# Rotary shuffle by transfers or by VectorE, and five smaller moves around it, in a hybrid decoder layer on one core

## The chip, the core and the metric

The kernel runs on one core of a Trainium2 chip. The core has five engines with instruction streams of their own: TensorE (PE: matrix products; PEld is its weight load), VectorE (DVE), ScalarE (ACT), GpSimd (POOL) and SyncE (SP, which here only issues DMA transfers). Each engine works through its instructions in order; semaphores order the engines among each other. SBUF is the memory of 128 partitions that engines work in, PSUM the small one that TensorE writes to. The metric is the device time of one execution in microseconds; less is better.

## The reference

One inference step of a one-layer decoder, for a prompt of 1024 positions and a sample group of 8 x 4 positions, with d = 1024. In short:

```python
xn = rms_norm(x, g_pre_mix)
h = xn @ w_in          # q_a k_a v_a | q_r k_r v_r | gate_r | gm_a gm_r
o_a = window_attn(rope_partial(q_a), rope_partial(k_a), v_a)      # window 128, sinks
qr, kr = rope_ret(q_r), rope_ret(k_r) * DK_R ** -0.5              # 4 heads, key 128, value 256
o_r, new_s = retention(qr, kr, v_r, s0)                           # chunks of 128, decaying state
y_a = o_a @ w_a_proj
y_r = (silu(gate_r) * head_rms(o_r)) @ w_r_proj
mixed = (sigmoid(gm_a) * y_a + sigmoid(gm_r) * y_r) @ w_o
x = x + rms_norm(mixed, g_post_mix)
f = conv_ffn(rms_norm(x, g_pre_ffn))                              # w_up, causal conv of 3, gelu * b, w_down
x = x + rms_norm(f, g_post_ffn)

def rope_ret(x, pos):
    ...
    x1 = x[..., ::2]
    x2 = x[..., 1::2]
    rot = jnp.stack([-x2, x1], axis=-1).reshape(x.shape)
    return x * cos + rot * sin
```

All is float32. Outputs are the new x of both groups, the last 128 keys and values, the retention states and the last two rows of the convolution's input.

## The kernel before

**Numbers and products.** Activations lie transposed, features on the partitions and the T = 1056 positions (32 of the sample, 1024 of the prompt) along the rows. A float32 product is made of three fast ones: both factors are split into a rounded part and a remainder (`split`, L228 on ScalarE for the rounded part, L223 on VectorE for the rest), and `mm3` (L255 to L257) multiplies high by high, high by low and low by high. The large products use Strassen's scheme in Winograd's form, seven quarter products (A11, A12, A22, S1 to S4) in place of eight; the sums of quarters it needs are made on VectorE. HW = T / 4 = 264 columns is a quarter's width.

**Order.** The program is written in the order of the text, but the framework orders each engine's instructions by a simulated timeline (`schedule_with_timeline_sim=True`) and their dependencies. `pin` keeps an instruction in program order with the other pinned ones; `PIN[0] = True` pins all splits. Transfers are issued by SyncE (`ld`) or GpSimd (`st`). `tpool` holds 16 tiles of (128, T), `wsp` three buffers each for `w_hi` and `w_lo`, `wraw` two raw weights.

**Stages**, with their times in the profiled execution:

- 0 to about 250: input norm, attention, the value projection of the retention.
- about 250 to 300: `attn_proj` (L779 to L787), the output projection of the attention; beside it `x_sums(0)` and `x_sums(1)` (L796) build the operands S2, S3, A22 and S1's of both halves of X for the input projection, and `first_weights` (L834) splits five of the first seven weights between the operand S2 and the operands S3 and A22 of half 1; these last are pinned. Then the pool `p2` is closed and `rs` opened in its place.
- `stream` (L901): a generator for the seven products of 16 pairs of column blocks of w_in, each for two halves of the positions. `adv(n)` takes n products of it; other stages call `adv` to mix their work with it. A22's product is made one half late. Each finished half (`pair`, a tile of (128, T): the two blocks beside each other) is handed to a `post`, which runs at `flush` after the S2 product of the next half.
- 300 to about 420, the sample stage: 18 products ahead, then `sample(h)` (L1024 to L1075) for the four heads, three products after each of its five parts. It reads the rotated q and k back from DRAM (`qk_d`), updates the states of the 8 sequences (`s0`, read by SyncE and written by GpSimd) and ends with two transposes (`turn`, L1012) of the normed result. The `post` of the first four pairs is `post_qk`, the retention's rotation: with q or k as x, `x * rcos + shuffled(x) * rsin`, where the shuffle swaps neighbouring partitions (L864), for two blocks of 128 x 528 a half.
- 420 to about 700, the prompt's retention: 32 blocks (`ahead`, `front`, `middle`, `tail`), four products of the stream in each. q and k of a block are loaded four blocks ahead (`load_qk`), five buffers. `tail` also makes eight quads of sums of w_r (`quad_load`, `quad_sums`), two for each head, at blocks 0, 2 and 3, 5, and writes them to `r_d`.
- 700 to about 803: the products with w_r, in the order PORD = A11, A12, S2, S3, A22, S1, S4. `z_done` (L1270) adds the results up in `Gr`, and `merge` (L1260) multiplies a finished quarter by its gate and adds the attention's part (L1267, L1268): GpSimd for row blocks 0 to 3, VectorE for 4 to 7. `merged_to_X` splits `Gr` back into X for half 0 after A22 and for half 1 at the end. In between the eight row blocks of w_o are loaded and split (`weights`, L246 and L223), blocks 2 to 6 into tiles of `tpool`, block 7 into `wsp`.
- 803 to about 918: the output projection w_o with its norms, nine row tiles; row tile 0 takes the blocks of w_o in the order LATE.
- 918 to the end: the FFN, pairs of w_up, convolution, gate, sums of w_down (`down_sums`) and products with w_down.

`NSPL` counts the split weights of a stream: each seventh goes to a tile of its own (`w7x`), the others alternate between the rings `hi` and `lo`.

The seam of the input projection in the text (L819 to L856), as far as the change touches it:

```python
    def x_sums(j):
        ...
        for p, src in ((S2, t2), (S3, t3), (A22, t)):
            if j and p == S3:
                first_weights()
                PIN[0] = True
            ex1[p, j] = [TT("ex", (P, 4, HW), F32R) for _ in range(2)]
            split(*ex1[p, j], src)
        PIN[0] = False
```

## Time and profile before

| what | us |
|---|---|
| median of 3 runs (1672.16 to 1676.08) | 1675.57 |
| the profiled execution | 1673.6 |
| its span, first to last instruction of the program | 1671.8 |

The profile is one execution. A group of instructions is given as line, engine, operation, tile written and tiles read, shape and count, then busy time, mean of one in ns, and the idle time of the engine before them with what ended it. A wait is given as who waited for whom, with the sum, the number and the longest. Idle time of an engine that does not set the pace costs nothing, and one that waits for several things is put down to the last.

### The profile page before, as it was taken

The page shows a single profiled execution, that of the slowest core. Times are in us where ns is not written, and L with a number is a line of the kernel's source. Part 1 is how long each engine was busy: PE and PEld are TensorE (multiplying, and loading weights), DVE is VectorE, ACT ScalarE, POOL GpSimd, SP SyncE. Part 2 cuts the span into 40 slices and gives each one's busy share as a digit, 9 for nine tenths or more (in the row PEclk, how much of TensorE's full clock was granted, in tenths as well). Part 3 has the DMA queues.
Part 4 walks back from the last instruction along what each step waited for, and adds up shares of the span by engine and source line. Part 5 has one row for each costly group of instructions (what it writes and reads, how often), then busy time and mean ns, then how long its engine had stood idle before and what let it go on. Part 6 is the DMA issues. An engine that isn't in the chain of part 4 may idle for free.

```text
span 1671.8 us, 32491 instructions
## 1 busy us (share of the span) xinstructions
PE 1629.8 (97%) x12551; PEld 1587.6 (95%) x12551; DVE 1229.3 (74%) x2035; ACT 860.4 (51%) x1882; POOL 474.1 (28%) x686
## 2 busy tenths in 40 slices
PE   8999999898999999999999999999999999999997
PEld 7999989888999999999688999999999999999997
DVE  7887738799556566478847988888898988455476
ACT  6565634355655655554333655555555556443343
POOL 4242430456343433250412122212322223111111
PEclk9999999999999999999999999999999999999999
DMA  7312232445676775597523144545444548866664
GB/s 199 67 46 72 70 78 99 151 137 170 211 243 217 239 236 178 186 296 213 186 89 103 51 142 159 172 147 172 159 160 160 173 158 257 243 192 195 195 187 144
DMA packets 273291, 273.88 MB, mean 164 GB/s; under 512 B 23040, under 2 KB 234272, under 8 KB 273121
## 3 DMA queue, kind: packets, MB, share of 16 engines
q1 hardware_dynamic: 239377, 155.25, 32.0%
q0 software_dynamic: 33760, 116.57, 20.1%
q8 instruction: 98, 1.61, 0.4%
q14 instruction: 56, 0.46, 0.1%
HBM read 184.24 MB, written 87.49 MB: 163 GB/s over the span
## 4 chain that ended last, share of the span: by engine, by line
PE 68%; DVE 3%; DMA 2%; issue 1%; ACT 1%; SPq 0%; POOL 0%; DVEq 0%; ACTq 0%; POOLq 0%
PE ps_m L257 9%; PE ps_m L256 9%; PE ps_m L255 9%; PE ps_t L256 8%; PE ps_t L255 8%; PE ps_t L257 8%; PE ps_q L255 4%; PE ps_q L257 4%; PE ps_q L256 4%; DVE xl L223 1%; DMA zt<-in_w_r_proj 1%; PE ps_b L1155 1%; PE ps_a L1159 1%; PE ps_b L1157 1%; PE ps_t L461 0%
## 5 line engine op out<-in xcount | busy, mean ns | idle before, releaser
L255 PE MATMUL ps_q<-xh,w 128*128 128x264 f32 x512 | 152.4, 298 | 5.4 <-DVE pair L949 3.0
L223 DVE SCALAR_TENSOR_TENSOR w_lo<-w_raw,w_hi 128x1024 fp32r<-128x1024 f32 x83 | 106.7, 1290 | 65.5 <-ACT w_hi L228 59.9
L255 PE MATMUL ps_t<-xh,w_hi 128*128 128x264 f32 (+2 forms) x524 | 149.0, 284 | 0.0
L256 PE MATMUL ps_t<-xl,w_hi 128*128 128x264 f32 (+2 forms) x524 | 148.9, 284 | 0.0
L257 PE MATMUL ps_t<-xh,w_lo 128*128 128x264 f32 (+2 forms) x524 | 148.2, 283 | 0.0
L257 PE MATMUL ps_m<-xh,w_lo 128*128 128x264 f32 x512 | 145.7, 285 | 0.5 <-DVE w_lo L223 0.5
L255 PE MATMUL ps_m<-xh,w_hi 128*128 128x264 f32 x512 | 146.0, 285 | 0.0
L256 PE MATMUL ps_q<-xl,w 128*128 128x264 f32 x512 | 145.9, 285 | 0.0
L256 PE MATMUL ps_m<-xl,w_hi 128*128 128x264 f32 x512 | 145.5, 284 | 0.0
L257 PE MATMUL ps_q<-xh,w 128*128 128x264 f32 x512 | 145.4, 284 | 0.0
L223 DVE SCALAR_TENSOR_TENSOR w<-w_raw,w 128x512 fp32r<-128x512 f32 x152 | 113.3, 751 | 36.9 <-ACT w L331 35.4
L1500 DVE SCALAR_TENSOR_TENSOR c_out<-u_ext,fconst,c_out 128x1024 f32<-128x1024 f32 x96 | 122.3, 1281 | 2.0 <-ACT c_out L1496 0.5
L228 ACT CAST w_hi<-w_raw 128x1024 fp32r<-128x1024 f32 x62 | 65.2, 1052 | 104.5 <-PE ps_t L256 75.0
L331 ACT CAST w<-w_raw 128x512 fp32r<-128x512 f32 x152 | 93.9, 622 | 37.9 <-DVE w_raw L223 22.9
L255 PEld LDWEIGHTS ps_q<-xh,w 128*128 128x128 f32 x512 | 96.6, 189 | 7.5 <-DVE pair L949 4.4
L257 PEld LDWEIGHTS ps_t<-xh,w_lo 128*128 128x128 f32 x524 | 98.8, 189 | 0.0
L255 PEld LDWEIGHTS ps_t<-xh,w_hi 128*128 128x128 f32 x524 | 98.7, 188 | 0.0
L256 PEld LDWEIGHTS ps_t<-xl,w_hi 128*128 128x128 f32 x524 | 98.7, 188 | 0.0
L257 PEld LDWEIGHTS ps_m<-xh,w_lo 128*128 128x128 f32 x512 | 96.4, 188 | 0.8 <-DVE w_lo L223 0.7
L256 PEld LDWEIGHTS ps_q<-xl,w 128*128 128x128 f32 x512 | 96.6, 189 | 0.5
L256 PEld LDWEIGHTS ps_m<-xl,w_hi 128*128 128x128 f32 x512 | 96.3, 188 | 0.0
L255 PEld LDWEIGHTS ps_m<-xh,w_hi 128*128 128x128 f32 x512 | 96.3, 188 | 0.0
(447 smaller groups left out, 6045.7 us busy)
## 6 DMA issues: line engine op xcount, KB each, us to landing
w_raw<-in_w_up SPq DMA_DIRECT2D x48, 512.0 KB, 4.1
w_raw<-in_w_in SPq DMA_DIRECT2D x42, 512.0 KB, 4.6
w_raw<-s_d SPq DMA_DIRECT2D x60, 256.0 KB, 4.0
t_d<-t POOLq DMA_DIRECT2D x24, 528.0 KB, 3.9
t<-t_d POOLq DMA_DIRECT2D x24, 528.0 KB, 5.1
t<-in_w_down SPq DMA_DIRECT2D x48, 256.0 KB, 4.4
s_d<-t POOLq DMA_DIRECT2D x24, 512.0 KB, 3.5
w_raw<-in_w_down SPq DMA_DIRECT2D x36, 256.0 KB, 5.7
```

The costliest lines, as they stand in the source:

```text
L223: pinned(V.scalar_tensor_tensor(out=out, in0=in0, scalar=1.0, in1=in1, op0=mult, op1=op))
L228: pinned(S.copy(out=hi, in_=src))
L255: TE.matmul(ps, wh, xh, start=start, stop=False, **kw)
L256: TE.matmul(ps, wh, xl, start=False, stop=False, **kw)
L257: TE.matmul(ps, wl, xh, start=False, stop=stop, **kw)
L331: S.copy(out=t[:, 0:4], in_=src)
L1155: TE.matmul(po, sT, vt, start=True, stop=tt == 0)
L1157: TE.matmul(po, q, state["s"], start=False, stop=True)
L1159: TE.matmul(pk, kt, vt, start=True, stop=True)
L1500: V.scalar_tensor_tensor(out=c[:, NS:], in0=u[:, g, NU + t:NU + t + SEQ], scalar=sc[t], in1=c[:, NS:], op0=mult, op1=add)
```

## The change

1. **Rotation.** In `post_qk` the two shuffles of VectorE become four transfers of SyncE inside SBUF, each of 64 of the 128 partitions (even to odd, odd to even), and the two elementwise instructions for each block that GpSimd did are done by VectorE.
2. **Start of the stream.** `first_weights` goes. `x_sums(1)` ends before the operands S3 and A22; four products of the stream are issued first, then these two operands (pinned), and then the pool is closed. In the first pair the weights of S3 and A22 are asked for after the products of S4 and S3. The ring of split weights is shifted by two (`NSPL` 2, and back to 0 for the FFN).
3. **Sums of w_r.** Four of the eight quads, those of column blocks 0 and 1, are made after `x_sums(1)` in two tiles of `p2`; `tail` makes one quad for each head.
4. **Sample stage.** 14 products ahead (with the four above, 18). The last copy of `sample`, with its two transposes, is issued after the next three products, the last one after two.
5. **Retention.** q and k are loaded three blocks ahead.
6. **Seam to w_o.** `merge` runs on VectorE for half 1 and on GpSimd for half 0. w_o's block 6 is split into `wsp` after the last w_r weights, ahead of block 7. Row tile 0 takes the blocks in plain order.
7. **FFN.** Four of the sums of w_down use the tile `t0` in place of `t2`.

```diff
-    NSPL = [0]
+    NSPL = [2]
...
         for p, src in ((S2, t2), (S3, t3), (A22, t)):
             if j and p == S3:
-                first_weights()
-                PIN[0] = True
-            ex1[p, j] = [TT("ex", (P, 4, HW), F32R) for _ in range(2)]
-            split(*ex1[p, j], src)
-        PIN[0] = False
+                return t3, t
+            operand(p, j, src)
+
+    def operand(p, j, src):
+
+        ex1[p, j] = [TT("ex", (P, 4, HW), F32R) for _ in range(2)]
+        split(*ex1[p, j], src)
...
     x_sums(0)
-    x_sums(1)
-
-    ph_stack.close()
-    rp = pool("rs", 1, stack=ph_stack)
+    late = x_sums(1)
+    for n in range(4):
+        t = quarters(p2.tile([P, T], F32, name="quad", bufs=2))
+        quad_load(w_r, n // 2, 0, n % 2, t)
+        quad_sums(r_d, n // 2, 0, n % 2, t)
...
             for i in range(2):
-                V.stream_shuffle(sh[i], both(o)[:, i], R_SHUF)
+                x = both(o)[:, i]
+                for b in range(2):
+                    ld.dma_start(out=sh[i][b::2], in_=x[1 - b::2])
             for i in range(2):
                 x = both(o)[:, i]
-                ew(G, x, x, c, mult)
+                ew(V, x, x, c, mult)
                 ew(V, sh[i], sh[i], d, mult)
-                ew(G, x, x, sh[i], add)
+                ew(V, x, x, sh[i], add)
...
-        ws = begun.pop()
-        ops = dict(begun)
-        ops[S3] = next(ws)
+        ws = in_split(ORDER[0])
+        next(ws)
+        next(ws)
+        ops = {p: next(ws) for p in EARLY[:5]}
...
-                        if j == 0:
+                        if j == 0 and i:
                             ops[A22] = next(ws)
...
+                    if p == S4 and S3 not in ops:
+                        ops[S3] = next(ws)
+                    if p == S3 and A22 not in ops:
+                        ops[A22] = next(ws)
+                        ws = coming
+                        next(ws)
...
+    adv(4)
+    PIN[0] = True
+    for p, t in zip((S3, A22), late):
+        operand(p, 1, t)
+    PIN[0] = False
+    ph_stack.close()
+    rp = pool("rs", 1, stack=ph_stack)
...
-        S.copy(out=z8[:, h], in_=turn(pt, finish(os8, NS, 1, h, 1)))
+        o = finish(os8, NS, 1, h, 1)
+        turns.append(lambda: S.copy(out=z8[:, h], in_=turn(pt, o)))
 
+    turns = []
     for n in range(2):
         load_s0(n)
-    adv(18)
+    adv(14)
     for h in range(4):
         for _ in sample(h):
             adv(3)
+            while turns:
+                turns.pop()()
+    adv(2)
+    turns.pop()()
...
-        if tt in (0, 3):
+        if tt == 0:
             quads[h] = quarters(ST("zt", (P, T), bufs=3))
-            quad_load(w_r, h, 0, tt // 3, quads[h])
-        if tt in (2, 5):
-            quad_sums(r_d, h, 0, tt // 3, quads.pop(h))
+            quad_load(w_r, 2 + h // 2, 0, h % 2, quads[h])
+        if tt == 2:
+            quad_sums(r_d, 2 + h // 2, 0, h % 2, quads.pop(h))
...
-        load_qk(g + 4)
+        load_qk(g + 3)
...
-        eng = G if m < 4 else V
+        eng = V if half else G
...
+    def out_weights(m):
+
+        wo.append(weights(1, D, [(lambda r: r[:, 0], w_o[m * P:(m + 1) * P, :])],
+                          [wop, wop, tpool, tpool, tpool, tpool, None, None][m]))
...
+            if pi == 6 and c == 0:
+                out_weights(6)
...
-        for m in {0: (0,), 1: (1,), 2: (2,), 3: (3, 4), 4: (5,), 5: (6,), 6: (7,)}.get(pi, ()):
-            wo.append(weights(1, D, [(lambda r: r[:, 0], w_o[m * P:(m + 1) * P, :])],
-                              [wop, wop, tpool, tpool, tpool, tpool, tpool, None][m]))
+        for m in {0: (0,), 1: (1,), 2: (2,), 3: (3, 4), 4: (5,), 6: (7,)}.get(pi, ()):
+            out_weights(m)
...
-    LATE = (0, 1, 2, 3, 4, 7, 5, 6)
+    LATE = range(KD)
...
+    NSPL[0] = 0
     prepare(2)
...
-            down_sums(20 + (i - 5) // 4, tr.tile([P, 4, HW], F32, name="t2"))
+            down_sums(20 + (i - 5) // 4, tr.tile([P, 4, HW], F32, name="t0"))
```

More of the change, by code (lines that the diff above doesn't have):

```diff
@@ L793, in trunk @@
     COLS += [(c, c + P) for b in (GR0, GA0, GM0) for c in range(b, b + D, 2 * P)]
-    begun = []
     def x_sums(j):
@@ L832, in in_split @@
         yield w_split(a22, V)
-    def first_weights():
-        ws = in_split(ORDER[0])
-        next(ws)
-        next(ws)
-        begun.extend((p, next(ws)) for p in EARLY[:5])
-        begun.append(ws)
     for mm in range(4):
@@ L1217, in ahead @@
             state["dm"] = mask(g // NB)
-        load_qk(g + 4)
+        load_qk(g + 3)
         load_v(g + 3)
         return front(g, state["dm"])
-    for g in range(4):
+    for g in range(3):
         load_qk(g)
@@ L1225, in trunk @@
         load_v(g)
+    adv(0)
     coming, behind = ahead(0), None
@@ L1239, in trunk @@
     tail(*behind)
-    adv(len(ORDER) * 14 - 8 - 78 - 4 * NBLK - 1)
+    adv(len(ORDER) * 14 - 8 - 80 - 4 * NBLK - 1)
     for n in range(4):
```

## The prediction

> **What bounds the kernel now.** I read the page first, then the stages (busy time of each engine in stretches of the span), then in the stages with an idle TensorE the waits, the groups of instructions and the timeline.
>
> ```profile
> span 1671.8 us, 32491 instructions
> PE 1629.8 (97%) x12551; PEld 1587.6 (95%) x12551; DVE 1229.3 (74%) x2035; ACT 860.4 (51%) x1882; POOL 474.1 (28%) x686
> ```
>
> TensorE is busy for 97%, and the change adds and removes no matmul. So it can win only idle TensorE time, 42 us in all, and only where it lies in stages that the change touches. The stages (stretch, length, busy us and count of PE, PEld, DVE, ACT, POOL, then clock and DMA):
>
> ```profile
> 250.00:300.00 50.00, 48.40 (x314) 48.18 (x314) 36.97 (x37) 22.61 (x41) 4.87 (x9) 1.00 0.24 91
> 300.00:420.00 120.00, 107.04 (x835) 101.86 (x836) 109.78 (x164) 58.98 (x159) 66.99 (x55) 1.00 0.50 157
> 420.00:700.00 280.00, 279.12 (x2161) 273.47 (x2160) 163.99 (x348) 161.54 (x392) 96.90 (x161) 1.00 0.68 213
> ...
> 800.00:820.00 20.00, 16.01 (x62) 12.43 (x61) 18.24 (x27) 8.13 (x20) 11.31 (x9) 0.91 0.71 213
> ...
> 920.00:1660.00 740.00, 740.00 (x6109) 739.61 (x6107) 575.79 (x907) 383.46 (x711) 156.99 (x262) 1.00 0.55 172
> ```
>
> Two places matter. The sample stage, 300 to 420, leaves TensorE idle for 120 - 107.0 = 13.0 us while VectorE is busy for 109.8 of 120: VectorE sets the pace. The seam between the w_r products and the w_o products, 800 to 820, leaves 4.0 us. The FFN (920 to 1660) has nothing to win and 164 us of slack on VectorE. TensorE's waits in the sample stage, then those around the seam (who waited for whom: us, times, longest):
>
> ```profile
> PE ps_b L1062 <- DVE s0s L223: 4.2, 7, 0.8
> PE ps_q L255 <- DVE pair L949: 3.0, 2, 1.8
> PE ps_q L255 <- ACT pair L926: 2.3, 1, 2.3
> PE ps_q L255 <- DVE pair L951: 2.1, 3, 0.9
> PE ps_b L1012 <- ACT o L1006: 1.3, 1, 1.3
> PE ps_a L1041 <- ACT r L1034: 1.0, 1, 1.0
> ```
>
> ```profile
> PE ps_m L256 <- DVE w_loT L223: 3.9, 1, 3.9
> ...
> PE ps_m L257 <- DVE w_lo L223: 0.5, 1, 0.5
> ```
>
> 9.3 of the first 13.9 us are waits for VectorE.
>
> **Term 1, the rotation (sample stage).** `post_qk` runs eight times (four heads, two halves), all of them in this stage. VectorE's groups here, and POOL's (count, then busy us, mean ns, idle before):
>
> ```profile
> L223 DVE SCALAR_TENSOR_TENSOR w<-w_raw,w 128x512 fp32r<-128x512 f32 x17 | 21.2, 1263 | 0.8 <-ACT w L331 0.8
> L223 DVE SCALAR_TENSOR_TENSOR sh<-sh,rsin 128x528 f32<-128x528 f32 x16 | 18.7, 1167 | 0.1
> L864 DVE STREAM_SHUFFLE sh<-pair 128x528 f32<-128x528 f32 x16 | 12.1, 758 | 0.0
> L223 DVE SCALAR_TENSOR_TENSOR s0s<-s,s0s 128x512 fp32r<-128x512 f32 x13 | 10.9, 841 | 0.0
> ...
> L223 DVE SCALAR_TENSOR_TENSOR w<-s,w 128x512 fp32r<-128x512 f32 x9 | 7.3, 812 | 1.2 <-ACT w L331 1.1
> ...
> L223 DVE SCALAR_TENSOR_TENSOR s<-w_raw 128x512 f32<-128x512 f32 x5 | 3.4, 689 | 3.8 <-DMA w_raw<-in_w_in 3.8
> ```
>
> ```profile
> L225 POOL TENSOR_TENSOR pair<-pair,sh 128x528 f32<-128x528 f32 x16 | 25.5, 1596 | 12.4 <-DVE sh L223 12.2
> L225 POOL TENSOR_TENSOR pair<-pair,rcos 128x528 f32<-128x528 f32 x16 | 25.1, 1567 | 28.1 <-DVE sh L864 20.3 <-DMA rcos<-in_rcos 7.8
> ```
>
> The same two shapes in the middle of the FFN, 1000 to 1300:
>
> ```profile
> L223 DVE SCALAR_TENSOR_TENSOR w<-w_raw,w 128x512 fp32r<-128x512 f32 x59 | 40.5, 686 | 7.9 <-ACT w L331 7.9
> ...
> L223 DVE SCALAR_TENSOR_TENSOR t<-c_out,t 128x528 f32<-128x528 f32 x16 | 11.2, 700 | 0.0
> ```
>
> One VectorE instruction that takes 700 ns there takes 1167 ns here. The timeline shows why; VectorE, then POOL:
>
> ```profile
> 321.78 0.70 DVE L223 SCALAR_TENSOR_TENSOR sh<-sh,rsin 128x528 f32<-128x528 f32 x1
> ...
> 324.73 1.82 DVE L223 SCALAR_TENSOR_TENSOR sh<-sh,rsin 128x528 f32<-128x528 f32 x1
> ```
>
> ```profile
> 324.22 1.77 POOL L225 TENSOR_TENSOR pair<-pair,rcos 128x528 f32<-128x528 f32 x1
> ```
>
> The first runs with POOL free; the second starts 0.51 us into a POOL instruction and ends 0.56 us after it. POOL's elementwise work holds up VectorE instructions that read two operands from SBUF. The excess in the quoted groups is 17 x (1263 - 686) = 9.8, 16 x (1167 - 700) = 7.5, 13 x (841 - 686) = 2.0 and 9 x (812 - 686) = 1.1, together 20.4 us, or 0.64 us for each of POOL's 32 instructions.
>
> The change takes POOL's 32 instructions away and does them on VectorE: +32 x 0.700 = +22.4. The 16 shuffles go: -12.1. The excess goes: -20.4. VectorE falls from 109.8 to 99.7 us. Beside its present idle time of 120 - 109.8 = 10.2 us that makes 109.9 us, close to TensorE's own 107.0.
>
> What it adds is a wait. Each post issues four transfers on SyncE (32 in all), SBUF to SBUF, 64 partitions and 132 KB each, and its VectorE instructions, the product with cos included since it overwrites what the transfers read, cannot start before they land. VectorE takes its instructions in order, so what is queued behind, the weight splits (`w_split`) and the evictions at L949 and L951, waits too, and TensorE for those. The trace of before has no such transfer; the nearest ones, and the load that VectorE meets in this stage (KB each, median us to landing):
>
> ```profile
> kS<-kS POOLq DMA_DIRECT2D x8, 96.0 KB, 2.8
> ...
> w_raw<-in_w_in SPq DMA_DIRECT2D x42, 512.0 KB, 4.6
> ```
>
> VectorE's wait is bounded below by nothing (other work stands ahead of it) and above by what it loses to the w_r quads in the next stage, quoted under term 3: 13.5 us in 6 waits, 2.25 each. Nearest is the load of w_raw here, 3.8 us over five first uses, 0.76 each, landing in 4.6 against 2.8; I take 0.5 a post, 4.0 us, and put half of it into idle time that exists already. The stage becomes 109.9 + 2.0 = 111.9: **-8.1 us**. Ends: -13.0 (all idle gone) to +7.9 (2.25 a post, none hidden: 109.9 + 18.0 - 120).
>
> Inside these 13.0 us lie two other parts. The 2.3 us for `ACT pair` fall where ScalarE casts the S3 and A22 operands of half 1 before it evicts; they now come after four products. The 1.3 us for `ACT o` are a sample transpose, now three products later. I count neither again. S3's and A22's own first weights now stand behind S4 and S3 in program order; the attention projection is the cover, and its loss is a rival below.
>
> **Term 2, the seam.** ScalarE at the cast of w_o block 6, and the stage just before:
>
> ```profile
> 806.13 1.05 ACT L246 CAST w_hiT<-w_raw 128x1024 fp32r<-128x1024 f32 x1 [2.77 <-DVE xl L223]
> ```
>
> ```profile
> 780.00:800.00 20.00, 20.00 (x155) 19.39 (x154) 20.00 (x40) 6.01 (x14) 3.57 (x2) 1.00 0.81 238
> ```
>
> Block 6 has tiles of the T pool, so its cast waits for a split of the merged rows, and TensorE 3.9 us for the pair. The change gives it buffers of the ring that the w_r weights use, free before the last products. Block 7 is then late next: it needs the buffer of the next to last w_r weights, but TensorE asks for it only as the last of eight. I take 3.4 of the 4.0 us idle: **-3.4 us**; ends 0 and -4.0. Two of the ring's three buffers stay taken until the last w_o product, so the second w_up weight of the first FFN pair splits late: 1.05 (the cast above) and 1.29 us,
>
> ```profile
> L223 DVE SCALAR_TENSOR_TENSOR w_lo<-w_raw,w_hi 128x1024 fp32r<-128x1024 f32 x83 | 106.7, 1290 | 65.5 <-ACT w_hi L228 59.9
> ```
>
> hidden by the first weight's 96 products at 740 / 6109 = 0.121 us, 11.6 us; without that cover +2.3.
>
> The merges keep their number on each engine, but A22's move to POOL (into a stretch where VectorE has no idle time) and S4's to VectorE. POOL's:
>
> ```profile
> L1267 POOL TENSOR_TENSOR Gr<-Gr,g_in x8: 1418/1731/2343, 732.3 to 808.7; 128x528 f32<-128x528 f32 x8
> ```
>
> At 0.64 us lost for each POOL instruction, A22's eight cost VectorE 5.1 and spare it 8 x 0.70 = 5.6; S4's do the reverse. I take 0.
>
> The Trainium skill (SBUF — State Buffer, section "SBUF: two separate sides") has GpSimd and VectorE take the shared ports by an exclusive lock, so that "the other fully blocks". Quoted as it stands it speaks against A22's merges on POOL: eight instructions of about 1.7 us would hold VectorE up to 13.8 us instead of 5.1, and the seam's gain would go. The pair of rows at 324 us agrees with the blocking, the mean of 0.64 us says that most of a POOL instruction passes while VectorE does something else.
>
> **Term 3, the sums of w_r.** Four of eight quads move from the retention blocks to a place before the stream. In the retention stage (420 to 700): the sums, VectorE's wait for their loads, TensorE's only wait.
>
> ```profile
> L223 DVE SCALAR_TENSOR_TENSOR zt<-zt 128x256 f32<-128x256 f32 x32 | 13.5, 423 | 14.6 <-DMA zt<-in_w_r_proj 13.5 <-DMA z_d<-zt 0.8
> ```
>
> ```profile
> DVE zt L223 <- DMA zt<-in_w_r_proj: 13.5, 6, 4.7
> ```
>
> ```profile
> PE ps_a L1142 <- DVE state L1162: 0.8, 1, 0.8
> ```
>
> Half the sums leave a stage in which TensorE idles for 0.9 us: **-0.4 us**. They add 16 x 0.423 = 6.8 us of VectorE, eight loads and four stores between 250 and 300, where VectorE idles for 13.0 us. Cost 0 by that cover; +6.8 without it.
>
> **At nothing:** q and k three blocks ahead instead of four (TensorE's only wait of the retention stage, quoted above, is not for them); the order of w_o blocks in row tile 0; the shifted ring of split weights; `t0` for `t2` in the FFN, under 164 us of slack.
>
> **Sum.** -8.1 - 3.4 - 0.4 = -11.9 us. The profiled execution took 1673.6 us (span 1671.8), so 1661.7; the median of the runs, 1675.57, lies 2.0 above it: **1663.7 us**.
>
> **Rivals.**
> - *Everything goes*: no new wait, all idle time of both places and the 0.8 us gone: -17.8, 1657.8. For it: VectorE would be at 99.7 of 107. Against: ScalarE's waits have other causes.
> - *The transfer takes the place of the contention*: VectorE loses 2.25 us a post as it does with w_r's quads, 18.0 us. Half hidden, the stage takes 118.9, unhidden 127.9; with the 3.8 of the other terms -4.9 to +4.1, 1670.7 to 1679.7. For it: both are small transfers met by an in-order engine.
> - *The stream opens late* (the edit does not do what it says): the sums of w_r stand ahead of the first weights on VectorE and the 13.0 us of idle time cannot be used. +6.8 on the forecast: 1670.5.
> - *Slower*: SyncE, too, works in order, and in this stage it stands before loads of the state until an earlier store has landed:
>
> ```profile
> SPq L1022 <- DMA out_ret_sample<-s: 52.4, 9, 12.7
> ```
>
> That is 52.4 of 120 us, 5.8 each. If transfers come at random, 44% of the posts, 3.5, stand behind such a wait: 20.3 us more on VectorE, stage 132.2, total +8.4: 1684.0. It decides for slower from 11.9 us of added waits on. The Trainium skill (DMA: Bandwidth & Descriptors, section "Anatomy of one DMA — SWDGE (gpsimd) path") says that a transfer's semaphore wait happens on the issuing sequencer before dispatch; SyncE's row agrees.
>
> **Chances.** Forecast 0.46 (own range 1658 to 1669), everything 0.11, transfer for contention 0.20, late opening 0.08, slower 0.15. About 0.3%, 5.0 us, is what a measurement of this kernel can tell from no change: under 1670.5 is faster, over 1680.6 slower. Faster: 0.46 + 0.11 + 0.04 + 0.04 = 0.65. Same: 0.16 + 0.04 + 0.01 = 0.21. Slower 0.14. The range goes from 1655, beyond the full gain, to 1680, the end of the second rival.
>
> **What would show it.** Term 1: VectorE's `w` and `sh` groups at about 690 to 700 ns, no POOL rotation, and TensorE idle in the sample stage 4 to 6 us instead of 13; wrong, if VectorE waits for `sh` over 1 us a post or SyncE stands before `sh`. Term 2: no wait for `w_loT`; wrong, if a wait for `w_lo` or for the evictions of the products takes its place between 770 and 815. Term 3: fewer waits for `zt`, and no new TensorE wait between 285 and 305. A TensorE idle time in the FFN would overturn the whole.

## The result: 0.65% faster, and the profile after

| | before | after |
|---|---|---|
| median of 6 runs each, us | 1675.82 (1672.16 to 1679.78) | 1664.93 (1661.43 to 1666.85) |
| ratio, 95% interval | | 0.9935 [0.992, 0.995] |
| the profiled execution, us | 1673.6 | 1666.58 |
| its span, us | 1671.8 | 1664.8 |
| the input projection's last product ends | 714.6 | 707.0 |
| from there to the last w_r product | 82.7 | 88.6 |
| from there to the last w_o product | 108.3 | 103.3 |

The change is faster by 10.9 us; forecast were 11.9 from the profiled execution and a time of 1663.7. The two profiled executions are only 7.0 apart, since the one of before lay 2.2 below its median and the one of after 1.7 above. The last three rows are read from TensorE's records of one execution each. They already say that not every term held: the input projection ends 7.6 us earlier, the stretch of w_r is 5.9 longer, that of w_o 5.0 shorter. The first lines of the page after:

```profile
span 1664.8 us, 32494 instructions
PE 1628.7 (98%) x12551; PEld 1588.7 (95%) x12551; DVE 1205.1 (72%) x2035; ACT 862.9 (52%) x1882; POOL 446.3 (27%) x654
```

The stages after, with the columns of before:

```profile
300.00:420.00 120.00, 112.43 (x902) 110.78 (x901) 95.45 (x168) 65.46 (x160) 18.04 (x25) 0.99 0.58 191
420.00:700.00 280.00, 278.62 (x2154) 272.63 (x2153) 159.78 (x335) 164.36 (x400) 95.69 (x158) 1.00 0.65 206
700.00:800.00 100.00, 94.21 (x740) 91.29 (x739) 74.47 (x101) 45.70 (x74) 37.35 (x28) 1.00 0.81 248
800.00:820.00 20.00, 20.00 (x87) 15.74 (x87) 15.09 (x32) 8.09 (x22) 2.95 (x6) 1.00 0.65 208
```

and the line for 700 to 800 of before, which the prediction didn't show:

```profile
700.00:800.00 100.00, 98.86 (x797) 97.72 (x796) 77.46 (x108) 50.30 (x81) 28.25 (x22) 1.00 0.85 262
```

TensorE's idle time in the sample stage falls from 13.0 to 120 - 112.4 = 7.6 us. The 4.0 us of the seam are gone from 800 to 820, but 700 to 800 has 5.8 idle where before had 1.1. VectorE's groups in the sample stage after, and its largest wait there:

```profile
L223 DVE SCALAR_TENSOR_TENSOR w<-w_raw,w 128x512 fp32r<-128x512 f32 x20 | 13.7, 686 | 1.8 <-ACT w L331 1.5
L223 DVE SCALAR_TENSOR_TENSOR pair<-pair,rcos 128x528 f32<-128x528 f32 x16 | 11.3, 704 | 14.6 <-DMA sh<-pair 14.6
...
L223 DVE SCALAR_TENSOR_TENSOR sh<-sh,rsin 128x528 f32<-128x528 f32 x16 | 11.2, 701 | 0.0
```

```profile
DVE pair L223 <- DMA sh<-pair: 14.6, 7, 4.0
```

The split `w` fell from 1263 to 686 ns and the product with sin from 1167 to 701, the lengths of the FFN: the hold by GpSimd is gone. The transfers are waited for 14.6 us in 7 waits, 2.1 us each; from issue to landing one takes 2.5 us (median of 32). TensorE's waits around the seam, 700 to 830:

```profile
PE ps_m L255 <- DVE Gr L1296: 1.5, 2, 1.3
PE ps_m L257 <- DVE w_lo L223: 1.1, 2, 0.8
PE ps_m L255 <- ACT w_hi L228: 1.1, 1, 1.1
PE ps_m L255 <- DVE Gr L1298: 1.0, 1, 1.0
PE ps_q L255 <- DVE pair L948: 0.6, 1, 0.6
PE ps_m L255 <- DVE Gr L1300: 0.5, 1, 0.5
```

One wait of 3.9 us for `w_loT` became a row of small ones for VectorE (the additions into `Gr`, the splits). The timeline shows where VectorE's time went; GpSimd's merges of A22, then VectorE:

```profile
774.63 1.45 POOL L1284 TENSOR_TENSOR Gr<-Gr,g_in 128x528 f32<-128x528 f32 x1 [1.50 <-DVE Gr L1298]
776.16 1.38 POOL L1285 TENSOR_TENSOR Gr<-Gr,a_in 128x528 f32<-128x528 f32 x1
...
781.50 2.18 POOL L1285 TENSOR_TENSOR Gr<-Gr,a_in 128x528 f32<-128x528 f32 x1
```

```profile
774.48 3.36 DVE L223 SCALAR_TENSOR_TENSOR xl<-Gr,xh 128x264 fp32r<-128x264 f32 x3
777.76 0.42 DVE L1298 TENSOR_TENSOR Gr<-ps_m,Gr 128x264 f32<-128x264 f32 x1
778.10 1.45 DVE L223 SCALAR_TENSOR_TENSOR xl<-Gr,xh 128x264 fp32r<-128x264 f32 x4
...
782.42 0.42 DVE L1296 TENSOR_TENSOR Gr<-ps_m,Gr 128x264 f32<-128x264 f32 x1
```

Four splits `xl` take 1.45 us with GpSimd idle; three take 3.36 while GpSimd makes two instructions in the same stretch. The addition into `Gr` at 777.76 waits behind them, and TensorE for it. The addition at 782.42, which reads PSUM, runs in the middle of a GpSimd instruction and keeps its 0.42 us.

### The profile page after: what moved, and what is told of

The parts are those of the page before. It is cut to its first block, busy times and chain, and to the rows that moved or that the text cites. A ratio compares the mean times of both kernels' runs of the same rounds, so it can differ in the third digit from the quotient of the medians.

```text
span 1664.8 us, 32494 instructions
## 1 busy us (share of the span) xinstructions
PE 1628.7 (98%) x12551; PEld 1588.7 (95%) x12551; DVE 1205.1 (72%) x2035; ACT 862.9 (52%) x1882; POOL 446.3 (27%) x654
## 4 chain that ended last, share of the span: by engine, by line
PE 84%; DVE 6%; DMA 5%; issue 3%; ACT 1%; POOL 0%; SPq 0%; DVEq 0%; POOLq 0%; ACTq 0%
PE ps_m L255 9%; PE ps_m L257 9%; PE ps_m L256 9%; PE ps_t L256 8%; PE ps_t L255 8%; PE ps_t L257 7%; PE ps_q L255 5%; PE ps_q L257 5%; PE ps_q L256 5%; PE ps_mm L255 3%; PE ps_mm L256 3%; PE ps_mm L257 3%; DMA sh<-pair 1%; DMA w_raw<-r_d 1%; PE ps_a L255 1%
## 5 line engine op out<-in xcount | busy, mean ns | idle before, releaser
L223 DVE SCALAR_TENSOR_TENSOR w<-w_raw,w 128x512 fp32r<-128x512 f32 x152 | 104.1, 685 | 35.0 <-ACT w L331 34.3
L228 ACT CAST w_hi<-w_raw 128x1024 fp32r<-128x1024 f32 x62 | 65.2, 1052 | 105.3 <-PE ps_t L256 75.3
L255 PE MATMUL ps_q<-xh,w 128*128 128x264 f32 x384 | 114.3, 298 | 5.5 <-DVE pair L946 5.4
L255 PE MATMUL ps_q<-ex,w 128*128 128x264 f32 x384 | 113.5, 296 | 0.6 <-DVE pair L948 0.6
L256 PE MATMUL ps_q<-xl,w 128*128 128x264 f32 x384 | 110.3, 287 | 0.0
L257 PE MATMUL ps_q<-ex,w 128*128 128x264 f32 x384 | 110.1, 287 | 0.0
L256 PE MATMUL ps_q<-ex,w 128*128 128x264 f32 x384 | 109.8, 286 | 0.0
L257 PE MATMUL ps_q<-xh,w 128*128 128x264 f32 x384 | 109.8, 286 | 0.0
```

Source lines behind the costliest of these rows:

```text
L223: pinned(V.scalar_tensor_tensor(out=out, in0=in0, scalar=1.0, in1=in1, op0=mult, op1=op))
L228: pinned(S.copy(out=hi, in_=src))
L255: TE.matmul(ps, wh, xh, start=start, stop=False, **kw)
L256: TE.matmul(ps, wh, xl, start=False, stop=False, **kw)
L257: TE.matmul(ps, wl, xh, start=False, stop=stop, **kw)
```

## The experiments

Every kernel was timed in five rounds against the kernel before. The columns: median, ratio to before, then from one profile TensorE's idle time in two stretches, the end of the input projection, and the stretches of w_r and w_o after it. The kernels ran in four sittings, each with runs of the kernel before beside them, whose median lay between 1674.9 and 1675.8; the ratio is to these runs, and is the better number where two kernels are close.

| kernel | median us | ratio [95%] | idle 300-420 | idle 420-700 | projection ends | w_r | w_o |
|---|---|---|---|---|---|---|---|
| before | 1675.8 | 1 | 13.0 | 0.9 | 714.6 | 82.7 | 108.3 |
| after | 1664.9 | 0.9935 [0.992, 0.995] | 7.6 | 1.4 | 707.0 | 88.6 | 103.3 |
| e3_rot_old | 1672.6 | 0.9988 [0.9979, 0.9997] | 11.4 | 2.1 | 712.7 | 87.9 | 103.3 |
| e4_rot_vec | 1664.8 | 0.9938 [0.9926, 0.9949] | 3.3 | 4.7 | 706.3 | 87.5 | 103.2 |
| e5_rot_gp | 1686.5 | 1.0066 [1.0054, 1.0078] | 16.8 | 5.0 | 725.0 | 87.9 | 103.3 |
| e6_rot_only | 1675.5 | 0.9998 [0.9989, 1.0007] | 5.2 | 10.5 | 715.8 | 82.9 | 109.1 |
| e12_before_vec | 1678.3 | 1.0017 [1.0003, 1.003] | 2.3 | 10.7 | 714.9 | 85.9 | 108.4 |
| e1_merge_old | 1662.1 | 0.9922 [0.991, 0.9935] | 5.0 | 1.8 | 703.3 | 84.4 | 105.3 |
| e2_wo_old | 1664.4 | 0.9929 [0.9916, 0.9943] | 6.6 | 2.9 | 706.7 | 88.0 | 106.2 |
| e7_vec_merge_old | 1662.0 | 0.9918 [0.9905, 0.9932] | 2.5 | 4.7 | 703.4 | 84.9 | 105.3 |
| e8_vec_merge_v | 1657.2 | 0.9888 [0.9874, 0.9901] | 2.7 | 2.7 | 700.6 | 82.7 | 102.4 |
| e9_sums_old | 1667.1 | 0.995 [0.9937, 0.9962] | 7.3 | 3.4 | 709.9 | 88.1 | 103.2 |
| e10_turn_old | 1662.9 | 0.9925 [0.9912, 0.9938] | 6.2 | 3.1 | 704.6 | 87.6 | 103.2 |
| e11_qk_four | 1665.5 | 0.9946 [0.9933, 0.9959] | 6.0 | 5.0 | 709.1 | 88.2 | 103.3 |

### What the rotation is worth in the changed kernel

**e3_rot_old**, the changed kernel with the old rotation:

```diff
-                x = both(o)[:, i]
-                for b in range(2):
-                    ld.dma_start(out=sh[i][b::2], in_=x[1 - b::2])
+                V.stream_shuffle(sh[i], both(o)[:, i], R_SHUF)
...
-                ew(V, x, x, c, mult)
+                ew(G, x, x, c, mult)
...
-                ew(V, x, x, sh[i], add)
+                ew(G, x, x, sh[i], add)
```

> The changed kernel with the rotation of before: two shuffles on VectorE and the four elementwise instructions on GpSimd. Theory: the rotation brought the gain of the sample stage, because GpSimd's 32 elementwise instructions no longer hold up VectorE's two-operand ones. Then VectorE's weight splits go back from 686 to about 1260 ns in the stage 300 to 420, the last product of the input projection comes at about 714 us instead of 707.0, and the kernel takes 7 to 9 us more than the changed one: about 1673 where before has 1675.8. Rival: the later operands and weights at the start of the stream and the later sample transposes brought it. Then the last product stays within 2 us of 707 and the kernel takes about 1666.

1672.6: 7.7 us are given back, and VectorE is held again. Its groups and the stage:

```profile
L223 DVE SCALAR_TENSOR_TENSOR sh<-sh,rsin 128x528 f32<-128x528 f32 x16 | 20.1, 1254 | 0.1
L223 DVE SCALAR_TENSOR_TENSOR w<-w_raw,w 128x512 fp32r<-128x512 f32 x17 | 17.6, 1037 | 0.8 <-ACT w L331 0.8
```

```profile
300.00:420.00 120.00, 108.65 (x855) 105.35 (x854) 109.56 (x165) 62.52 (x162) 68.49 (x57) 0.99 0.49 156
```

With everything else of the change in place, the rotation is worth 7.7 us by the medians (8.9 by the ratios), next to the 8.1 of the forecast. In the two profiles the input projection ends 5.7 us later than in the change, 712.7 against 707.0.

**e4_rot_vec**, the changed kernel with the shuffle on VectorE and GpSimd out all the same (as e3_rot_old, with `V` in place of `G`), and **e5_rot_gp**, the transfers kept and the two elementwise instructions back on GpSimd (`ew(G, x, x, ...)`):

> The changed kernel with the shuffle on VectorE again, but the elementwise instructions on VectorE as in the changed one: no transfers, no GpSimd. VectorE gets 16 x 0.76 = 12.1 us more than in the changed kernel (95.5 becomes 107.6 us of 120) and loses the 14.6 us in which it waits for the transfers. Theory (GpSimd's hold on VectorE is what cost the stage, and the transfers are worth little): the stage stays as in the changed kernel, last product of the input projection at 707 plus or minus 2, kernel within 3 us of the changed one, about 1662 to 1668. Rival (taking the shuffle off VectorE is what counts): 5 us or more are lost, 1670 or more.

> The changed kernel with the transfers, but the elementwise instructions on GpSimd again. VectorE is freed of 12.1 us of shuffles and of 32 instructions, but is held up by GpSimd as in before. Theory: the hold of some 20 us comes back (weight splits at about 1200 ns in the sample stage), VectorE still has less to do than before (109.8 - 12.1 = 97.7 us), and the last product comes at 709 to 713; kernel 1667 to 1672. Rival (count of VectorE work alone decides): VectorE has 22.4 us less to do than in the changed kernel and the stage gets shorter: last product at 705 or earlier, kernel under 1664.

e4 takes 1664.8, the time of the change: the transfers as such bring nothing, and the gain is GpSimd's absence. Here 12.1 us of shuffles and 14.6 us of waits for transfers come to the same time. e5 takes 1686.5, slower than before and far above what was expected of it. It pays both prices; its wait for the transfers, and its groups, in the sample stage:

```profile
DVE sh L223 <- DMA sh<-pair: 15.3, 8, 3.9
```

```profile
L223 DVE SCALAR_TENSOR_TENSOR sh<-sh,rsin 128x528 f32<-128x528 f32 x16 | 17.4, 1085 | 15.4 <-DMA sh<-pair 15.3
L223 DVE SCALAR_TENSOR_TENSOR w<-w_raw,w 128x512 fp32r<-128x512 f32 x16 | 16.9, 1053 | 1.2 <-ACT w L331 1.1
```

### What the rotation is worth alone

**e6_rot_only**, the kernel before with the new rotation, and **e12_before_vec**, the kernel before with all of the rotation on VectorE and no transfers. The diff of the first (the second keeps `stream_shuffle`):

```diff
             for i in range(2):
-                V.stream_shuffle(sh[i], both(o)[:, i], R_SHUF)
+                x = both(o)[:, i]
+                for b in range(2):
+                    ld.dma_start(out=sh[i][b::2], in_=x[1 - b::2])
             for i in range(2):
                 x = both(o)[:, i]
-                ew(G, x, x, c, mult)
+                ew(V, x, x, c, mult)
                 ew(V, sh[i], sh[i], d, mult)
-                ew(G, x, x, sh[i], add)
+                ew(V, x, x, sh[i], add)
```

> The kernel before with the changed rotation alone (transfers, elementwise instructions on VectorE). Theory: the rotation is the whole of the gain, so the last product of the input projection comes at 705 to 708 us instead of 714.6, and with the seam of before (191.2 us from there to the last product with w_o) the kernel takes 7 to 9 us less than before: 1666 to 1668, ratio about 0.995. Rival: the rotation brings it only together with the later operands and sample transposes (TensorE's waits for ScalarE of 2.3 and 1.3 us stay): 3 to 5 us less, 1670 to 1672.

> The kernel before with all of the rotation on VectorE, the shuffle included, and no transfers. Theory A (the new rotation alone gained nothing because its 32 transfers stand on the loads' queue ahead of the first q and k): without them the wait for q and k is gone and the sample stage's gain stays, 1666 to 1670. Theory B (what the rotation frees is given back at the joint to the retention whoever moves the rows, since the projection's products for that joint have been used up earlier): again 8 to 11 us idle of TensorE between 420 and 700 us, 1673 to 1677.

1675.5 and 1678.3: no gain at all, and both theories for e6 are missed. Yet the sample stage does what the prediction says. The stages of e6, then of e12:

```profile
300.00:420.00 120.00, 114.78 (x926) 112.55 (x927) 95.67 (x171) 67.10 (x170) 17.74 (x24) 1.00 0.62 201
...
420.00:700.00 280.00, 269.55 (x2065) 263.11 (x2064) 158.99 (x339) 155.27 (x381) 97.32 (x160) 0.99 0.66 209
```

```profile
300.00:420.00 120.00, 117.73 (x959) 116.53 (x960) 106.26 (x203) 68.88 (x173) 22.10 (x26) 1.00 0.57 175
420.00:500.00 80.00, 70.75 (x502) 67.73 (x502) 40.72 (x86) 40.08 (x102) 25.76 (x43) 0.91 0.65 206
```

The idle time of 300 to 420 falls from 13.0 to 5.2 and 2.3 us, and 420 to 700 gets 10.5 and 10.7 where before had 0.9. The products of the input projection show how. The view by stretches for the tile `ps_q` alone, before, then e12 (the count beside PE is what to read; it counts matmuls, twelve of which make one product of the stream):

```profile
250.00:450.00 200.00, 135.08 (x1008) 127.43 (x1008) 10.04 (x24) 21.47 (x59) 1.00 0.46 151
450.00:500.00 50.00, 41.80 (x292) 37.49 (x292) 2.59 (x6) 6.64 (x18) 1.00 0.78 240
```

```profile
250.00:450.00 200.00, 148.49 (x1129) 142.09 (x1129) 10.93 (x26) 24.64 (x67) 1.00 0.50 160
450.00:500.00 50.00, 31.23 (x181) 26.92 (x182) 1.71 (x4) 3.73 (x11) 0.86 0.63 199
```

At 450 us e12 is 121 matmuls ahead, about ten products; at 500 only 1310 - 1300 = 10 matmuls. The sample's last product on the state ends at 439.0 (437.8 before) and the first product of q and k starts at 449.7 (449.9): the sample's own chain is no shorter. What VectorE's free time does is to let projection products run earlier, between the sample's steps; at the joint to the retention fewer of them are left to run between its first blocks, and TensorE waits there. TensorE's waits from 420 to 500, e12, then e6:

```profile
PE ps_a L1142 <- DVE state L1162: 4.4, 1, 4.4
PE ps_q L255 <- ACT pair L926: 2.9, 1, 2.9
PE ps_b L1012 <- ACT o L1006: 1.8, 1, 1.8
```

```profile
PE ps_a L1144 <- DMA qk<-qk_d: 2.9, 1, 2.9
PE ps_b L1014 <- ACT o L1008: 2.8, 1, 2.8
PE ps_q L255 <- DVE pair L953: 2.4, 1, 2.4
PE ps_a L1144 <- DVE state L1164: 1.5, 1, 1.5
```

The wait for q and k is gone without the transfers, the loss is not. So the idle time that theory B of e12 names is there, 10.7 us, with a time even 1.3 us above its range: the gain is handed back at the joint, whoever moves the rows. (That e12 is slower than before doesn't come from here: its projection ends 0.3 us later, its stretch of w_r is 3.2 us longer.)

Behind these waits stand loads. The chain of e12 that ended last, followed back from 500 us, has a load of weights before the wait near 458 us and a load of a gate before the one near 484 (start, then us to the landing):

```profile
444.21 12.73 DMA w_raw<-in_w_in
...
474.85 7.08 DMA zt<-gm_d
```

VectorE waits 8.3 us for this load of weights. In before it waits 4.3 us for one at the same place, up to 455.7 us, and TensorE, with products to do, idles for 0.1 us in all from 420 to 500. Nor is it enough for a loss that the products run early. e4 has the rotation of e12, and the same view of it reads:

```profile
250.00:450.00 200.00, 148.94 (x1142) 143.55 (x1143) 10.91 (x26) 24.84 (x67) 1.00 0.56 179
450.00:500.00 50.00, 35.83 (x226) 30.81 (x224) 2.58 (x6) 5.13 (x14) 0.93 0.64 203
```

It is 134 matmuls ahead of before at 450 us, further than e12, and still 68 at 500, with 4.7 us idle. That early products and a late load meet in e12 is shown; why they don't in e4 is not.

The six kernels side by side. The first number is the end of the input projection, the second the median:

| rotation | all else as before | all else as after |
|---|---|---|
| shuffle on VectorE, arithmetic on GpSimd | 714.6 / 1675.8 | 712.7 / 1672.6 |
| transfers, arithmetic on VectorE | 715.8 / 1675.5 | 707.0 / 1664.9 |
| all on VectorE | 714.9 / 1678.3 | 706.3 / 1664.8 |

The rotation alone is worth 0.3 us, the rest alone 3.2 (2.0 by its ratio), both 10.9. The 7.7 us are there only with the rest.

### Which part of the rest carries the joint

**e9_sums_old** makes all eight w_r quads beside the retention, as before; **e10_turn_old** issues the sample's transposes at once; **e11_qk_four** loads q and k four blocks ahead. Each is the changed kernel with one edit undone in the text:

```diff
e9_sums_old
-    for n in range(4):
-        t = quarters(p2.tile([P, T], F32, name="quad", bufs=2))
...
-        if tt == 0:
+        if tt in (0, 3):
...
-        if tt == 2:
+        if tt in (2, 5):
e10_turn_old
-        o = finish(os8, NS, 1, h, 1)
-        turns.append(lambda: S.copy(out=z8[:, h], in_=turn(pt, o)))
+        S.copy(out=z8[:, h], in_=turn(pt, finish(os8, NS, 1, h, 1)))
e11_qk_four
-        load_qk(g + 3)
+        load_qk(g + 4)
...
-    for g in range(3):
+    for g in range(4):
         load_qk(g)
```

> The changed kernel with all eight sums of w_r beside the retention, as before. Theory of the prediction (the four sums that moved are worth 0.4 us, beside a TensorE that has its operands): within 2 us of the changed kernel, 1663 to 1667. Rival (the sums ahead of the input projection's VectorE work delay its first products, and the retention has room): 2 to 4 us faster, 1661 to 1663. Second rival (the retention's queue cannot take eight loads of 256 KB beside three q and k loads): VectorE waits again for the loads of w_r between 420 and 700 us, and 3 us or more come on top, 1668 and more.

> The changed kernel with the sample's transpose issued at once by TensorE, as before, and not three products later. Theory from the run of the new rotation alone (each joint holds back part of what the rotation gives, the transpose 1.3 us to 2.8 us of it): TensorE waits again for ScalarE's o between 300 and 490 us, four times at most, and the time is 1 to 5 us longer, 1666 to 1670. Rival (the three products only change places with the wait): no wait longer than 1 us and the time of the changed kernel, 1664 to 1666.

> The changed kernel with q and k loaded four blocks ahead, as before, so four loads ahead of the first block. Theory from the run of the new rotation alone (the fourth load stands ahead of what the first block needs, TensorE waited 2.9 us for q and k there): a wait of TensorE for q and k of 1 to 4 us near 450 us, and 1665.5 to 1669. Theory of the prediction (the edit is worth nothing): no such wait, 1664 to 1666.

1667.1, 1662.9 and 1665.5. The change has 0.9935 [0.992, 0.995], and the intervals of all three overlap it. Both theories from e6 are missed, but two of the edits did not do what they were meant to. In e10 every engine has the instructions of the changed kernel in the same order, from the first to the last (operation, tiles and shape; buffer numbers and semaphores are not in this comparison). The framework places the sample's transposes alike in all three kernels: between the last product on the state and the transposes of a head stand 45 to 54 matmuls of the projection in before, 48 to 53 in the change and in e10. So e10 undoes nothing that can be seen, and its 2.0 us less, a projection that ends 2.3 us earlier and a wait of 2.0 us for ScalarE's `o` show how far two kernels of one order lie apart. e11 has the order of the change up to 558 us, so at the joint it undoes nothing either. Only e9 changes the order there: it lies 2.2 above the change, with 7.6 us of waits for `zt` back on VectorE, too little to separate from it. The later opening of the stream (point 2 of the change), with two products more ahead of the retention (4 + 14 + 60 + 2 = 80 in place of 18 + 60 = 78), was not undone alone; which part of the rest carries the joint **stays open**.

### The seam

**e1_merge_old** (the changed kernel with the merges of before), **e7_vec_merge_old** (e4 with them) and **e8_vec_merge_v** (e4 with all merges on VectorE):

```diff
e1_merge_old, e7_vec_merge_old
-        eng = V if half else G
+        eng = G if m < 4 else V
e8_vec_merge_v
-        eng = V if half else G
+        eng = V
```

> The changed kernel with the merges as before: GpSimd for row blocks 0 to 3, VectorE for 4 to 7, so A22's merges are on VectorE again and S4's on GpSimd. In the changed kernel the products with w_r take 88.7 us (706.8 to 795.6) against 82.9 before. Theory: A22's merges on GpSimd hold up VectorE between 767 and 784, and TensorE waits for its evictions (778 and 783 us, 2.3 us); with them back the products take 84 to 86 us and the kernel 3 to 5 us less than the changed one, about 1661. Rival: the loss comes from the new buffers of w_o's block 6 and the order of the loads (waits at 749 to 750 us): the products still take 88 us or more and the time is that of the changed kernel, or longer, since S4's merges return to GpSimd.

> The changed kernel without transfers (shuffles and elementwise instructions on VectorE) and with the merges as before. If the two edits add up, each as measured alone (the first equal to the changed kernel, the second 2.8 us less): 1661 to 1663. Rival: the 2.8 us came from another order of the instructions in the input projection (its last product came 3.7 us earlier there although nothing of it was changed), and that needs the transfers: then this one takes 1664 to 1666, with the last product of the input projection at 706 or later.

> The changed kernel without transfers and with all merges on VectorE: GpSimd does no elementwise work of 128 x 528 any more. VectorE gets 16 x 0.70 = 11.2 us more work in the seam and loses about 11.1 us of being held up. Theory (the hold at the wrong moment is what makes TensorE wait in the seam): the waits at 749, 774, 778 and 783 us go, the products with w_r take 82 to 84 us and those with w_o about 103.5, the kernel 1658 to 1661. Rival (VectorE's sum of work in the seam decides): nothing is won, products with w_r at 86 us or more, 1663 or more.

The stretch of w_r measures the merges: 88.6 in the change, 84.4 and 84.9 with the old ones, 82.7 with all of them on VectorE. For e8 the stage, and TensorE's only waits from 690 to 830:

```profile
700.00:800.00 100.00, 99.37 (x750) 95.98 (x750) 81.63 (x137) 50.08 (x85) 13.13 (x11) 1.00 0.84 263
```

```profile
PE ps_m L257 <- DVE w_lo L223: 0.6, 1, 0.6
PE ps_q L255 <- DVE pair L946: 0.6, 1, 0.6
```

VectorE does 16 instructions more than in e4 and TensorE waits less. **e8 beats both kernels**: 1657.2, ratio 0.9888 [0.9874, 0.9901], 7.8 us under the change. Its median is 7.6 us under that of e4; in the two profiles 5.7 us lie in the stretches w_r and w_o together (190.7 and 185.0), and another 5.6 in an input projection that ends earlier although nothing there was edited. For e1 and e7 the median falls by about 3, with intervals that overlap those of the change and of e4; only 2.2 and 0.5 us lie in these stretches, and the input projection ends 3.7 and 2.9 us earlier. The order of the instructions is no cause of that: on every engine it is the same up to 763 us in the change and e1, up to 764 in e4 and e7, up to 721 in e4 and e8.

**e2_wo_old**, the changed kernel with block 6 of w_o in the T pool, and the old order in row tile 0:

```diff
-                          [wop, wop, tpool, tpool, tpool, tpool, None, None][m]))
+                          [wop, wop, tpool, tpool, tpool, tpool, tpool, None][m]))
...
-    LATE = range(KD)
+    LATE = (0, 1, 2, 3, 4, 7, 5, 6)
```

> The changed kernel with w_o's block 6 in tiles of the T pool again, and the old order of blocks in row tile 0. Theory: the wait of 3.9 us for the low part of block 6 comes back; the time from the first to the last product with w_o is 107 to 108.5 us instead of 103.4, and the kernel takes 3 to 5 us more than the changed one, 1668 to 1670. Rival: the tiles it needs come free earlier now, because S4's merges are on VectorE; then the stage takes 103.5 to 105 us and the kernel stays within 2 us of the changed one.

1664.4, no difference to the change: the theory's 3 to 5 us more did not come, and of its waits only a part. Of the 3.9 us for `w_loT` 1.1 come back, with 2.2 for the last additions into `Gr`:

```profile
PE ps_m L255 <- DVE Gr L1300: 2.2, 1, 2.2
...
PE ps_m L256 <- DVE w_loT L223: 1.1, 1, 1.1
```

Block 6 in the ring, with the plain order, is worth 2.3 us in the profile (194.1 against 191.8 for both stretches) and none that the runs can tell.

## Why the prediction was right, and which steps failed

**The time.** 1664.9 against 1663.7, close, and in part by luck. In the two profiled executions the terms come to -7.6 + 0.8 = -6.8 us of the 11.9; the medians, 10.9 apart, differ by more because of where these two executions lie among the others. And what the medians have beside the rotation's 7.7 us, 3.2 by e3 (2.0 by its ratio), does not come from the seam that was to bring 3.4: from the end of the projection to the last w_o product e3 takes 191.2 us, before 191.0. It comes with a projection that ends 1.9 us earlier (714.6 and 712.7), for which the prediction had no term.

**Term 1, -8.1 us: right in mechanism and near in size, but only with the rest of the change.** GpSimd's hold was the cause (e3: 7.7 us, the `w` and `sh` groups back at 1037 and 1254 ns; e4: same time without transfers). Two of its quantities were off and cancelled in part. The wait for the transfers was taken at 0.5 us a post, 4.0 in all, and is 14.6, or 1.8 a post. By the prediction's own sign (over 1 us a post) that part was wrong: little else covered the 2.5 us that a transfer takes to land. It is near the 18.0 of the second rival, whose time didn't come all the same. One reason is that the hold was larger than the 20.4 us of the four groups counted, and VectorE's busy time fell to 95.5 and not 99.7: `v` from `vs` and `v` (L1038, now L1048) fell from 901 to 415 ns, `s` from `s` and `w_raw` from 945 to 686. But busy and waiting together are 95.5 + 14.6 = 110.1 of 120, against 99.7 + 4.0 = 103.7 forecast, and TensorE's idle time in the stage ended at 7.6, above the 4 to 6 that was to show it. The projection's end came 7.6 us earlier, 5.7 of it by the rotation (e3). The rival *slower* didn't come, though SyncE did stand before the transfers, 23.6 us in all, most of it until their input was written: its waits for the states fell from 52.4 to

```profile
SPq L1032 <- DMA out_ret_sample<-s: 26.7, 7, 9.0
```

**"At nothing": the step that failed most.** The joints were costed at nothing, or as two waits inside the 13.0 us. By e6 and e12 the idle time of the sample stage is not time gained until the next stage can take it: without the rest of the change term 1 is worth 0.3 us in place of 8.1. Idle time was read as if the stages stood one after the other, while projection products float between them. What had to be asked is what TensorE would do at 450 us with ten products fewer in hand while a load is late. That the rest of the change makes up for it was not foreseen, and by which of its parts is not known. The transposes, counted as moved by three products, were not moved (e10).

**Term 2, -3.4 us: failed.** The wait for `w_loT` went, and the stretch of w_o is 5.0 us shorter, more than the 3.4. But the stretch of w_r is 5.9 longer: together 191.0 became 191.8, +0.8. The prediction's sign of being wrong, a wait for `w_lo` or for the evictions in its place, came. Measured each by undoing it, block 6 with its order is worth 2.3 us (e2) and not 3.4, and the merges cost 2.2 (e1) or 0.5 (e7) and not 0. The step that failed is "I take 0" for the merges. That VectorE spares with A22 about what it loses is said of its busy time, not of who waits: A22's merges on GpSimd hold the splits, and with them the additions behind on which the next products wait, in a stretch where VectorE has no idle time. With all merges on VectorE (e8) w_r takes 82.7. The Trainium skill (SBUF — State Buffer, section "SBUF: two separate sides") had spoken against this edit, and is borne out in kind. Its rule is narrower than "GpSimd against VectorE": it names VectorE instructions in a two-port mode, or with two inputs in SBUF against a GpSimd instruction that reads SBUF. The timeline agrees: the splits `xl` are held, the addition with a PSUM input is not.

**Term 3, -0.4 us: not to be told.** Its signs came: VectorE's waits for `zt` from w_r fell from 13.5 to 0.7 us, and TensorE has no wait between 285 and 305. But TensorE's idle time from 420 to 700 is 1.4 us and not under 0.9, and e9 costs 2.2 us with overlapping intervals. The rival *late opening* (+6.8) is refuted: from 250 to 300 TensorE is busy for 48.7 us, before for 48.4, and the projection ends earlier, not later.

**The FFN** stayed as it was: from the last w_o product to the end of TensorE's work 756.2 and 756.5 us.

## What to carry to other kernels

Idle time taken out of one stage is gained only if the work that moves up was not what filled the next stage; count the filler's products at the joint, before and after, and look at the loads there, and not only the idle time. In this kernel the rotation and the merges were worth taking off GpSimd altogether, and not to another place: e8 gives VectorE 48 instructions more than before (2083 against 2035) and is the fastest. Test an edit both alone and undone: the rotation was worth 0.3 us the one way and 7.7 the other. And where a framework orders the instructions, read in the trace whether an undone edit has changed the order: e10 had not.

## What was not expected of the hardware

- GpSimd's elementwise instruction doesn't hold every VectorE instruction: three `xl` splits that need some 1.1 us (three quarters of the 1.45 for four) took 3.36 across two GpSimd instructions, while an addition that reads PSUM kept its 0.42 us beside a third one.
- A stall costs more than its length. In e12 TensorE waits 2.9 us near 458 us and 4.4 near 484. The stretches around the first (PE's busy time, then the granted clock, DMA share and GB/s):

```profile
456.00:458.00 2.00, 0.09 (x1) 0.87 0.13 33
458.00:460.00 2.00, 2.00 (x5) 0.50 0.00 0
...
462.00:464.00 2.00, 2.00 (x8) 0.50 0.00 0
464.00:466.00 2.00, 2.00 (x17) 0.92 0.73 187
```

  The clock goes to 0.50 and stays there for 6 us in which TensorE has work; after the second wait for 4 us more. Half of these 10 us, about 5, is an estimate of what is lost on top of the waits. How much of it reaches the end of the projection is not shown: by idle time, 2.3 + 10.7 us from 300 to 700 against 13.0 + 0.9 before, e12 would end it 0.9 us earlier, and it ends it 0.3 later. The Trainium skill (TensorE: Matmul & The Clock Gate, section "What's actually happening") has the clock fall to half after an idle window of about 3.4 us, and rise again after as long a busy one. The halving agrees, and so does the length: up to the end of the FFN every stretch at 0.50 in these traces lasts 3.4 or 6.8 us. But the window need not be idle. In e4 a wait of 2.0 us, up to 472.5 us, was enough. With the 13 traces that have such a fall cut into stretches of 3.41 us in step with it, all 19 at full clock in which TensorE was busy for 1.5 us or less end in a fall, and of those with more only three (1.77, 1.77 and 1.91 us).
- Kernels of one order differ. e10 has the order of the change on every engine, and its median is 2.0 us lower; e1 has it up to 763 us, and its input projection ended 3.7 us earlier in the profile. Differences of this size between two single profiles are not put down to an edit unless the stretch itself shows it.
